# Last partial sum of the first MLP in two passes: the context tokens, then the latents

## The chip, the cores and the metric

The kernel runs on one core of a Trainium2 chip. The core has a matrix engine (TensorE, PE in the rows, with PEld for its weight loads), VectorE (DVE), ScalarE (ACT), GpSimd (POOL) and SyncE (SP), which here issues the loads from memory. The engines work side by side; each takes its own instructions strictly in the order in which they stand in its queue, and they wait for each other through semaphores. The metric is device time in microseconds (us), the median of a few runs.

## The reference, cut to what matters

Two layers over 512 latent tokens and 256 context tokens of width 1024. The first layer's token mixer is a state-space mixer (SSD), the second's a neighbourhood attention in which the latents also read the context.

```python
# layer 0 ends, for the latents x and for the context ctx:
h2 = modulate(rmsnorm(t, g[2]), m[3], m[4])
t  = t + m[5] * rmsnorm(square(relu(h2 @ w1)) @ w2, g[3])       # t is x, or ctx
# layer 1 begins:
h  = modulate(rmsnorm(x,   g[0]), m_lat[0], m_lat[1])
hc = modulate(rmsnorm(ctx, g[0]), m_ctx[0], m_ctx[1])
q, k, v    = h  @ w_qkv                                         # latents
qc, kc, vc = hc @ w_qkv                                         # context: kc and vc are read by the latents
```

## The kernel before

Activations stand with the channels on the partitions: `ya` and `xa` (sub-layer output and residual stream) are 128 x 8 blocks x 768 columns, of which columns 0 to 511 are the latents and 512 to 767 the context (`SEG`, `PARTS`). Every product is made of three matmuls, high part by high part, low by high and high by low (`hh`/`hl`, `ah`/`al` are the two parts of the activations, `wh`/`wl` those of the weights). A weight unit of 128 x 1024 is loaded by SP (`wload`, L112) into one of three buffers and split by ACT (`wh`, L119) and DVE (`wl`, L120) into one of two buffers for each part.

The MLP goes over four quarters `c` of the hidden width: eight hidden blocks (L902), then the second matrix (L954), whose partial sums are added into `ya` by DVE (L960). An accumulator `acc` holds 768 columns, and there are two of them, so the matmuls of one output block can't begin before L960 has emptied the accumulator of the block two before it. In the last quarter each of the eight output blocks also feeds `sums.add`: ACT squares (L299, L306), a scaling by ACT (L389), a product by DVE (L305), and three running sums `syy`, `ssqy`, `sxy` on POOL (L309). After the eighth block `after0` follows:

- `sums.factors` adds over the channels by matmuls with ones (L263), and makes two normalising factors on small row tiles: `R` of the MLP's output, then `r` of the new stream, each by a chain of DVE and ACT instructions (L321, L246 to L250, L334 to L338) that ends in `rows` (L250), a matmul that spreads the row over the partitions (L274) and a copy into `syy` or `sxy` (L275).
- For each of the eight blocks, latents and context: `ya *= R`, `xa += ya` (L351, L352; three of the eight blocks on POOL), then scale and shift into `hh` and `hl`. For the context that is L356 and L358 on DVE and L357 on ACT; for the latents L999 and L1003 on DVE and L1000 and L1002 on ACT (in another column order).

Two chunks of modulation weights (`mod_chunk`, L169, with transposes L186) are worked in meanwhile. The attention then begins with pair `p == 0`: six tiles of values V (four of latents, two of the context; L1174) and the queries Q (L1170) in one loop over the weight halves `q` and blocks `k`, then keys (L1048).

The order within each engine's queue is set when the program is built, by a list scheduler that follows the program's order as priority, with exceptions marked `tc.high_priority()`. On the chip it is fixed.

Two other places already work in passes over columns: the SSD output projection (L144 with L872 in the place of L960), which does the context's 256 columns of all eight blocks, then the latents' 512, with `factors` and the norm of the context (`join`: L351, L352, L377, L378) running during the second pass; and the last MLP, in two halves of 256.

Of the kernel before, what the change touches and what calls it, by code (L numbers as in the profile page):

```python
# [10 lines left out]
ALU = mybir.AluOpType  # L11
AX = mybir.AxisListType

P = 128
D = 1024
KB = D // P
LAT = 512
CTX = 256
T = LAT + CTX
NCH = T // P  # L20
# [31 lines left out]
def trunk(ctx: ExitStack, tc: tile.TileContext, a, out, dbg=None, stop=None):  # L52
# [183 lines left out]
    def scaled(name, l, n, i, plus1):  # L236

        t = const.tile([P, KB, 2], F32, name=name)
        for o in (0, 4):
            scaled_half(t, l, n, i, plus1, o)  # L240
        return t
# [155 lines left out]
    hh, hl = h_tiles()  # L397
# [583 lines left out]
    def between0(c, o, mp):  # L981
        if c == 2 and o == KB - 1:
            G3[0] = scaled("G3", 0, 3, 5, False)

    def after0(i):

        nonlocal hh, hl
        A4 = scaled("A4", 1, 0, 1, True)
        hh, hl = h_tiles()
        sums.factors((0, 1, 2))  # L990
        for k in range(KB):
            for s, sl in enumerate(PARTS):
                sh = mod(1, 0, s)
                add_block(k, ya, xa, sums.R(sl), sl)
                b = ya[:, k, sl]
                if s == 1:
                    modulate(k, b, xa[:, k, sl], sums.r(sl), A4, sh, s, hh[:, k, sl], hl[:, k, sl])
                    continue
                dve.scalar_tensor_tensor(b, xa[:, k, sl], A4[:, k, s:s + 1], sums.r(sl), ALU.mult, ALU.mult)  # L999
                act.activation(b, b, AF.Identity, bias=sh[:, k:k + 1], scale=1.0)  # L1000
                for (bv, _), (_, hv), (_, lv) in zip(slots(b), slots(hh[:, k, sl]), slots(hl[:, k, sl])):
                    act.activation(hv, bv, AF.Copy)  # L1002
                    dve.tensor_tensor(lv, bv, hv.bitcast(F32), ALU.subtract)  # L1003

    segs1 = [(0, LAT, 0), (LAT, T + 2, LAT)]
    mlp(0, SEG, segs1, [segs1[1:], segs1[:1]], [(0, T)], [(0, 10), (0, 11)] + [(1, ch) for ch in (0, 1, 2, 3, 6, 7, 8, 9)], hh, hl, ya, xa, G3,
        between0, after0)
    for ch in (4, 5):
        mod_chunk(1, ch)
# [9 lines left out]
    with tc.tile_pool(name="na", bufs=1) as na:  # L1019
# [138 lines left out]
        for p in range(8):  # L1158
            even = p % 2 == 0
            acc = sps("a")  # L1160
            if p == 0:

                vacc = [sps("a"), sps("a"), sps("sc"), sps("sc"), sps("pt"), sps("yp")]
                ws = wqk.next()
                for q in range(2):
                    w = wv.next()
                    for k2 in range(4):
                        k = q * 4 + k2
                        for j, (ww, xx) in enumerate(((0, hh), (0, hl), (1, hh))):
                            pe.matmul(acc, lhsT=ws[ww][:, k * P:(k + 1) * P], rhs=xx[:, k, :LAT],  # L1170
                                      start=k == 0 and j == 0, stop=k == KB - 1 and j == 2)
                        for i in range(NCH):
                            for n, (xx, ww) in enumerate(((hh, 0), (hh, 1), (hl, 0))):
                                pe.matmul(vacc[i][:, :256], lhsT=xx[:, k, i * P:(i + 1) * P], rhs=w[ww][:, k2 * 256:k2 * 256 + 256],  # L1174
                                          start=k == 0 and n == 0, stop=k == KB - 1 and n == 2)
                for i in range(NCH):
                    v_out(0, vacc[i], i, 1)
            else:
                gemm([acc], SEG[:1], 3 if even else 0, 6 if even else 4)

            Q = [na.tile([P, LAT], F32R, tag=f"q{q}", name=f"q{q}", bufs=2) for q in range(2)]
            Q += qlow[p % 2]
            for o, i, n in ((0, 64, 448), (448, 0, 64)):
                for par in range(2):
                    own = half(par)
                    for to in (own, half(1 - par)):
                        act.activation(Q[par][to, o:o + n], acc[own, i:i + n], AF.Copy, scale=0.125)
                    dve.scalar_tensor_tensor(Q[2 + par][own, o:o + n], acc[own, i:i + n], 0.125, Q[par][own, o:o + n].bitcast(F32),
                                             ALU.mult, ALU.subtract)
            accs = [sps("a"), sps("a")]  # L1190
            gemm(accs, SEG, 0, 11 if even else 5)

            K = [na.tile([P, 896], F32R, tag=f"k{q}", name=f"k{q}", bufs=2) for q in range(2)]
            for acc, k0, n in zip(accs, (0, 640), (512, 256)):
                for par in range(2):
                    own = half(par)
                    act.activation(K[par][own, k0:k0 + n], acc[own, :n], AF.Copy)
                    dve.tensor_tensor(K[par][half(1 - par), k0:k0 + n], acc[own, :n], K[par][own, k0:k0 + n].bitcast(F32), ALU.subtract)
            for k in K:
                pool.tensor_copy(k[:, 512:640], k[:, :128].bitcast(F32))  # L1200
            step(1000)
            pending = attend(p, Q, K)
            if even and p:
                values_of(p)
# [164 lines left out]
```

## Time and profile before

| | |
|---|---|
| median of 3 runs | 2187.4 us (2185.53 to 2195.42) |
| profiled execution | 2191.73 us, its span 2189.9 us |
| busy: PE, PEld | 2073.0 us (95%), 1733.5 us (79%) |
| busy: DVE, ACT, POOL | 1278.6 us (58%), 1008.4 us (46%), 514.3 us (23%) |
| mean granted clock of TensorE | 0.975 |

The span runs from the first to the last instruction; 1.8 us of the profiled execution's time lie outside it. Times in the rows below count from the span's start. Matmuls overlap, so the step from one start to the next says how long one takes, and its own length is longer.

### The profile page before, as it was taken

To read this page: it belongs to the slowest core of one execution; us is meant where nothing else is said; L and a number is where in the kernel's file an instruction comes from. 1 tells how busy PE (TensorE), PEld (TensorE's weight loads), DVE (VectorE), ACT (ScalarE), POOL (GpSimd) and SP (SyncE) were. 2 spreads that over 40 slices of the span, in tenths; PEclk is the share of its full clock that TensorE was granted. 3 is DMA by queue.
4 is the path that set the end of the run, shared out by engine and by line. 5 is a ranking of instruction groups with operands and counts; after the bars stand their busy time and mean duration, and the time that the engine had idled before them with its cause. 6 is when DMAs were issued, how large, how long until landed. Compare 5 with 4: busy or idle time off the path is not lost.

```text
span 2189.9 us, 32496 instructions
## 1 busy us (share of the span) xinstructions
PE 2073.0 (95%) x12848; PEld 1733.5 (79%) x12848; DVE 1278.6 (58%) x2023; ACT 1008.4 (46%) x1751; POOL 514.3 (23%) x486
## 2 busy tenths in 40 slices
PE   6999998999999888999999999889999989999996
PEld 3777876878878766888888888668898768889895
DVE  5657968576683687314334244488777664345356
ACT  4565756567473553213223133356556643323244
POOL 0004435254451462000000001633222260000004
PEclk8999999999999999999999999989999989999998
DMA  6446758357676422333333111321111114222233
GB/s 253 135 152 187 234 158 238 115 173 221 192 200 235 156 74 85 107 114 116 116 116 114 59 59 68 106 78 50 56 54 54 49 50 155 95 97 87 97 107 115
DMA packets 93868, 269.72 MB, mean 123 GB/s; under 512 B 13074, under 2 KB 21652, under 8 KB 93716
## 3 DMA queue, kind: packets, MB, share of 16 engines
q1 hardware_dynamic: 85268, 242.47, 34.0%
q0 software_dynamic: 8448, 25.18, 4.4%
q8 instruction: 101, 1.65, 0.3%
q14 instruction: 51, 0.42, 0.1%
HBM read 244.27 MB, written 23.33 MB: 122 GB/s over the span
## 4 chain that ended last, share of the span: by engine, by line
PE 79%; DVE 9%; ACT 4%; DMA 3%; issue 2%; POOL 2%; SPq 0%; DVEq 0%; ACTq 0%; POOLq 0%
PE acc L902 21%; PE acc L144 21%; PE acc L954 20%; PE a L1048 4%; DMA E<-crow 2%; PE s L169 2%; PE a L1059 2%; PE yp L1134 1%; PE s L629 1%; DVE wl L120 1%; PE s L708 1%; PE pt L1119 1%; PE s L724 1%; PE s L263 1%; ACT wh L119 1%
## 5 line engine op out<-in xcount | busy, mean ns | idle before, releaser
L119 ACT ACTIVATE wh<-raw 128x1024 fp32r<-128x1024 f32 (+1 forms) x241 | 254.2, 1055 | 686.7 <-PE acc L954 309.7
L120 DVE TENSOR_TENSOR wl<-raw,wh 128x1024 fp32r<-128x1024 f32 (+1 forms) x241 | 301.9, 1253 | 255.1 <-ACT wh L119 248.6
L144 PE MATMUL acc<-hh,wh 128*128 128x512 f32 (+1 forms) x976 | 286.2, 370 | 7.8 <-ACT wh L119 3.0
L144 PE MATMUL acc<-hl,wh 128*128 128x512 f32 (+1 forms) x976 | 264.1, 346 | 0.5 <-DVE hl L762 0.5
L144 PE MATMUL acc<-hh,wl 128*128 128x512 f32 (+1 forms) x976 | 262.6, 344 | 2.0 <-DVE wl L120 2.0
L902 PE MATMUL acc<-hh,wh 128*128 128x258 f32 (+2 forms) x1024 | 242.8, 317 | 9.5 <-ACT hh L377 9.5
L954 PE MATMUL acc<-ah,wh 128*128 128x512 f32 (+1 forms) x832 | 247.4, 347 | 4.1 <-DVE ya L960 4.0
L902 PE MATMUL acc<-hl,wh 128*128 128x258 f32 (+2 forms) x1024 | 241.8, 314 | 3.9 <-DVE hl L378 3.8
L954 PE MATMUL acc<-ah,wl 128*128 128x512 f32 (+1 forms) x832 | 244.5, 343 | 0.8 <-DVE wl L120 0.8
L954 PE MATMUL acc<-al,wh 128*128 128x512 f32 (+1 forms) x832 | 244.8, 344 | 0.0
L902 PE MATMUL acc<-hh,wl 128*128 128x258 f32 (+2 forms) x1024 | 240.8, 313 | 0.0
L144 PEld LDWEIGHTS acc<-hh,wh 128*128 128x128 f32 (+1 forms) x976 | 155.2, 190 | 60.9 <-issue 38.3
L902 PEld LDWEIGHTS acc<-hh,wh 128*128 128x128 f32 x1024 | 160.9, 191 | 33.5 <-issue 11.5
L309 POOL TENSOR_TENSOR syy<-syy,last 128x512 f32<-128x512 f32 (+2 forms) x24 | 38.3, 1596 | 585.6 <-ACT last L299 585.5
L144 PEld LDWEIGHTS acc<-hh,wl 128*128 128x128 f32 (+1 forms) x976 | 153.7, 190 | 27.5 <-DVE wl L120 2.5
L902 PEld LDWEIGHTS acc<-hl,wh 128*128 128x128 f32 x1024 | 161.2, 191 | 17.9 <-DVE hl L378 5.9
L144 PEld LDWEIGHTS acc<-hl,wh 128*128 128x128 f32 (+1 forms) x976 | 154.2, 190 | 25.3 <-DVE hl L762 1.1
L902 PEld LDWEIGHTS acc<-hh,wl 128*128 128x128 f32 x1024 | 161.8, 191 | 11.6 <-DVE wl L120 0.4
L954 PEld LDWEIGHTS acc<-ah,wh 128*128 128x128 f32 x832 | 139.4, 189 | 32.7 <-issue 13.1
L954 PEld LDWEIGHTS acc<-ah,wl 128*128 128x128 f32 x832 | 139.6, 189 | 21.9 <-DVE wl L120 1.0
L954 PEld LDWEIGHTS acc<-al,wh 128*128 128x128 f32 x832 | 139.5, 189 | 20.0
L960 DVE TENSOR_TENSOR ya<-ya,acc 128x768 f32<-128x768 f32 (+2 forms) x56 | 40.6, 726 | 196.1 <-PE acc L954 196.1
(320 smaller groups left out, 3813.0 us busy)
## 6 DMA issues: line engine op xcount, KB each, us to landing
raw<-in_w_dram SPq DMA_DIRECT2D x136, 512.0 KB, 3.4
mraw<-in_modw_dram SPq DMA_DIRECT2D x72, 512.0 KB, 3.3
raw<-in_win_dram SPq DMA_DIRECT2D x48, 512.0 KB, 4.0
E<-crow SPq DMA_DIRECT2D x96, 256.0 KB, 5.0
eb<-erow POOLq DMA_DIRECT2D x96, 128.0 KB, 5.5
raw<-in_wout_dram SPq DMA_DIRECT2D x24, 512.0 KB, 3.7
raw<-in_modw_dram SPq DMA_DIRECT2D x8, 1024.0 KB, 17.8
raw<-in_wqk_dram SPq DMA_DIRECT2D x16, 512.0 KB, 3.3
```

Of the source, the lines that this page charges most:

```text
L119: act.activation(wh[:, :n], raw[:, :n], AF.Copy)
L120: dve.tensor_tensor(wl[:, :n], raw[:, :n], wh[:, :n].bitcast(F32), ALU.subtract)
L144: pe.matmul(acc[:m, s0:s1], lhsT=ww[:, i * m:(i + 1) * m], rhs=xx[:, k, s0:s1], start=first and i == 0 and j == 0, stop=last and i == len( ...
L169: mm = pe.matmul(ps[32 * j:32 * j + 32, hf * 256:hf * 256 + 256], lhsT=cact[:, 8 * kg + 2 * j:8 * kg + 2 * j + 32], rhs=raw[:, j * 256:j * ...
L263: pe.matmul(ps[32 * j:32 * j + 32], lhsT=ones[:, :32], rhs=t[i], start=i == 0, stop=i == len(t) - 1)
L309: pool.tensor_tensor(t[:, s0:s1], t[:, s0:s1], d, ALU.add)
L629: pe.matmul(ps, lhsT=btok[:, d, c], rhs=xw.rearrange("p e q -> p (e q)"), start=True, stop=True)
L902: pe.matmul(acc[:, d0:d0 + s1 - s0], lhsT=ww[wi], rhs=xx[:, k, s0:s1], start=k == 0 and j == 0, stop=k == KB - 1 and j == 2)
L954: pe.matmul(acc[:, s0:s1], lhsT=ww[:, k * P:(k + 1) * P], rhs=xx[:, s0:s1], start=k == 0 and j == 0, stop=k == KB - 1 and j == 2)
L960: dve.tensor_tensor(y, y, acc[:, p0:p1], ALU.add)
L1048: pe.matmul(acc[:, :s1 - s0], lhsT=ws[ww][:, k * P:(k + 1) * P], rhs=xx[:, k, s0:s1], start=k == 0 and j == 0, stop=k == KB - 1 and j == 2)
L1059: pe.matmul(acc, lhsT=xx[:, k, i * P:(i + 1) * P], rhs=w[ww][:, sl], start=k == 0 and n == 0, stop=k == KB - 1 and n == 2)
```

## The change

`after0` is called twice in layer 0. The last quarter's second matrix is done first for the 256 context columns of all eight output blocks, then for the 512 latent columns; its eight weight units are loaded and split a second time. After the first pass, the context's factors and norm are issued, after the second the latents'. `factors` is issued with priority. In the attention's first loop, the two context tiles of V are computed first in each half of the weights.

```diff
@@ -982,28 +982,32 @@
         if c == 2 and o == KB - 1:
             G3[0] = scaled("G3", 0, 3, 5, False)
 
+    A4 = [None]
+
     def after0(i):
 
         nonlocal hh, hl
-        A4 = scaled("A4", 1, 0, 1, True)
-        hh, hl = h_tiles()
-        sums.factors((0, 1, 2))
+        if i == 0:
+            A4[0] = scaled("A4", 1, 0, 1, True)
+            hh, hl = h_tiles()
+        with tc.high_priority():
+            sums.factors(((2,), (0, 1))[i])
         for k in range(KB):
-            for s, sl in enumerate(PARTS):
+            for s, sl in ((1 - i, PARTS[1 - i]),):
                 sh = mod(1, 0, s)
                 add_block(k, ya, xa, sums.R(sl), sl)
                 b = ya[:, k, sl]
                 if s == 1:
-                    modulate(k, b, xa[:, k, sl], sums.r(sl), A4, sh, s, hh[:, k, sl], hl[:, k, sl])
+                    modulate(k, b, xa[:, k, sl], sums.r(sl), A4[0], sh, s, hh[:, k, sl], hl[:, k, sl])
                     continue
-                dve.scalar_tensor_tensor(b, xa[:, k, sl], A4[:, k, s:s + 1], sums.r(sl), ALU.mult, ALU.mult)
+                dve.scalar_tensor_tensor(b, xa[:, k, sl], A4[0][:, k, s:s + 1], sums.r(sl), ALU.mult, ALU.mult)
                 act.activation(b, b, AF.Identity, bias=sh[:, k:k + 1], scale=1.0)
                 for (bv, _), (_, hv), (_, lv) in zip(slots(b), slots(hh[:, k, sl]), slots(hl[:, k, sl])):
                     act.activation(hv, bv, AF.Copy)
                     dve.tensor_tensor(lv, bv, hv.bitcast(F32), ALU.subtract)
 
     segs1 = [(0, LAT, 0), (LAT, T + 2, LAT)]
-    mlp(0, SEG, segs1, [segs1[1:], segs1[:1]], [(0, T)], [(0, 10), (0, 11)] + [(1, ch) for ch in (0, 1, 2, 3, 6, 7, 8, 9)], hh, hl, ya, xa, G3,
+    mlp(0, SEG, segs1, [segs1[1:], segs1[:1]], SEG[::-1], [(0, 10), (0, 11)] + [(1, ch) for ch in (0, 1, 2, 3, 6, 7, 8, 9)], hh, hl, ya, xa, G3,
         between0, after0)
     for ch in (4, 5):
         mod_chunk(1, ch)
@@ -1161,15 +1165,21 @@
             if p == 0:
 
                 vacc = [sps("a"), sps("a"), sps("sc"), sps("sc"), sps("pt"), sps("yp")]
-                ws = wqk.next()
                 for q in range(2):
                     w = wv.next()
+                    ws = ws if q else wqk.next()
+                    for i in (4, 5):
+                        for k2 in range(4):
+                            k = q * 4 + k2
+                            for n, (xx, ww) in enumerate(((hh, 0), (hh, 1), (hl, 0))):
+                                pe.matmul(vacc[i][:, :256], lhsT=xx[:, k, i * P:(i + 1) * P], rhs=w[ww][:, k2 * 256:k2 * 256 + 256],
+                                          start=k == 0 and n == 0, stop=k == KB - 1 and n == 2)
                     for k2 in range(4):
                         k = q * 4 + k2
                         for j, (ww, xx) in enumerate(((0, hh), (0, hl), (1, hh))):
                             pe.matmul(acc, lhsT=ws[ww][:, k * P:(k + 1) * P], rhs=xx[:, k, :LAT],
                                       start=k == 0 and j == 0, stop=k == KB - 1 and j == 2)
-                        for i in range(NCH):
+                        for i in range(4):
                             for n, (xx, ww) in enumerate(((hh, 0), (hh, 1), (hl, 0))):
                                 pe.matmul(vacc[i][:, :256], lhsT=xx[:, k, i * P:(i + 1) * P], rhs=w[ww][:, k2 * 256:k2 * 256 + 256],
                                           start=k == 0 and n == 0, stop=k == KB - 1 and n == 2)
```

Two places in the queues. The first is on DVE. Before, in the last quarter of the MLP, the emptying of one accumulator (L960), a weight split (L120) and the product of the sums (L305) follow each other, block after block:

```order
L305 TENSOR_TENSOR sxy_6161<-xa_6158,ya_6159 128x768
L960 TENSOR_TENSOR ya_6159<-ya_6159,acc_11073 128x768
L120 TENSOR_TENSOR wl_11205<-raw_11202,wh_11204 128x1024
L305 TENSOR_TENSOR last1_6162<-xa_6158,ya_6159 128x768
L960 TENSOR_TENSOR ya_6159<-ya_6159,acc_11137 128x768
L120 TENSOR_TENSOR wl_11269<-raw_11266,wh_11268 128x1024
L305 TENSOR_TENSOR last1_6162<-xa_6158,ya_6159 128x768
```

With the change, this stands in the second pass, where the accumulators of latent blocks 1, 2 and 3 are acc_11433, acc_11472 and acc_11511 (that of block 0, acc_11397, is emptied before the context's second factor; acc_11511 takes the buffer of acc_11433):

```order
L351 TENSOR_TENSOR ya_6159<-ya_6159,syy_6160 128x256
L120 TENSOR_TENSOR wl_11554<-raw_11551,wh_11553 128x1024
L358 SCALAR_TENSOR_TENSOR hl_11322<-ya_6159,modc_91,hh_11321 128x256 x2
L352 TENSOR_TENSOR xa_6158<-xa_6158,ya_6159 128x256
L305 TENSOR_TENSOR sxy_6161<-xa_6158,ya_6159 128x512
L356 SCALAR_TENSOR_TENSOR ya_6159<-xa_6158,A4_11318,sxy_6161 128x256
L960 TENSOR_TENSOR ya_6159<-ya_6159,acc_11433 128x512
L358 SCALAR_TENSOR_TENSOR hl_11322<-ya_6159,modc_91,hh_11321 128x256
L960 TENSOR_TENSOR ya_6159<-ya_6159,acc_11472 128x512
L305 TENSOR_TENSOR last1_6162<-xa_6158,ya_6159 128x512 x2
L960 TENSOR_TENSOR ya_6159<-ya_6159,acc_11511 128x512
```

The last context blocks' scale and shift (L356, L358), a weight split and the first latent product now stand in front of the L960 that empties the accumulator of latent block 1. In front of these rows, and behind the `rows` (L250) of the context's second factor, stand one more L120, seven L356 and five L358.

The second place is on PE, at the end of the MLP. Before: the matmuls that spread the second factor (L274, from `rows`), the transposes of the modulation, then the first of V, in which context and latent tiles take turns (pt and yp hold context tiles, sc and a latent ones):

```order
L169 MATMUL acc_11722<-raw_11741,cact_86 32x256 x4
L274 MATMUL s_11572<-rows_6164,sel_81 128x256
L274 MATMUL s_11575<-rows_6164,sel_81 128x256
L274 MATMUL s_11578<-rows_6164,sel_81 128x256
L186 MATMUL acc_11686<-consts_77,row_11711 128x128 x2
L186 MATMUL acc_11686<-consts_77,row_11715 128x128 x2
L186 MATMUL acc_11722<-consts_77,row_11747 128x128 x2
L186 MATMUL acc_11722<-consts_77,row_11751 128x128 x2
L1174 MATMUL pt_11793<-wh_11803,hh_11521 128x256
L1174 MATMUL pt_11793<-wl_11804,hh_11521 128x256
L1174 MATMUL yp_11794<-wh_11803,hh_11521 128x256
```

With the change, with L1175 for the context tiles of V:

```order
L274 MATMUL s_11728<-rows_6164,sel_81 128x256
L169 MATMUL acc_11850<-raw_11857,cact_86 32x256 x4
L169 MATMUL acc_11850<-raw_11863,cact_86 32x256 x4
L169 MATMUL acc_11850<-raw2_11869,cact_86 32x256 x4
L274 MATMUL s_11743<-rows_6164,sel_81 128x256
L274 MATMUL s_11746<-rows_6164,sel_81 128x256
L186 MATMUL acc_11814<-consts_77,row_11839 128x128 x2
L1175 MATMUL pt_11921<-wh_11925,hh_11321 128x256
L1175 MATMUL pt_11921<-wl_11926,hh_11321 128x256
L1175 MATMUL pt_11921<-wh_11925,hl_11322 128x256
L186 MATMUL acc_11814<-consts_77,row_11843 128x128 x2
```

The context tiles come first, and they, too, stand behind the L274 of the latents' second factor; there are two L274 for each factor instead of three.

## Rows read from the trace of the kernel before

**Rows 1.** Stretches: us, busy by engine (instructions), granted clock, DMA share, GB/s.

```profile
1336.65:1404.50 67.85, 67.85 (x387) 58.73 (x389) 27.77 (x26) 28.83 (x38) 35.81 (x18) 1.00 0.17 55
1404.50:1424.90 20.40, 10.16 (x106) 5.23 (x106) 15.38 (x21) 6.35 (x12) 12.61 (x12) 0.71 0.58 206
1424.90:1462.05 37.15, 29.16 (x183) 24.75 (x183) 34.95 (x68) 21.88 (x50) 12.71 (x11) 0.84 0.25 70
730.00:745.00 15.00, 12.23 (x100) 11.43 (x100) 10.92 (x15) 12.63 (x21) 10.86 (x10) 1.00 0.38 128
```

**Rows 2.** Chain that ended last, 1330 to 1500: start, us, what.

```profile
1424.48 0.42 DVE rows L250
...
1433.51 0.79 PE pt L1174 x2
```

**Rows 3.** Context's instructions on DVE, 1424 to 1462: busy us, mean ns.

```profile
L356 DVE SCALAR_TENSOR_TENSOR ya<-xa,A,sxy 128x256 f32<-128x256 f32 x8 | 5.2, 671 | 0.0
...
L358 DVE SCALAR_TENSOR_TENSOR hl<-ya,modc,hh 128x256 fp32r<-128x256 f32 x8 | 4.2, 527 | 0.0
...
L351 DVE TENSOR_TENSOR ya<-ya,syy 128x256 f32<-128x256 f32 x4 | 2.2, 550 | 0.0
...
L352 DVE TENSOR_TENSOR xa<-xa,ya 128x256 f32<-128x256 f32 x4 | 1.7, 417 | 0.0
```

**Rows 4.** PE in time, SSD output projection: start, us, [idle before <- releaser].

```profile
744.15 0.39 PE L144 MATMUL acc<-yh,wl 128*128 128x256 f32 x1 [0.26 <-DVE wl L120]
...
747.40 0.38 PE L144 MATMUL acc<-yh,wl 128*128 128x256 f32 x1 [0.25 <-DVE wl L120]
...
751.93 0.62 PE L263 MATMUL s<-syy,ones 128*32 128x256 f32 x2 [1.75 <-POOL syy L309]
...
753.35 0.50 PE L144 MATMUL acc<-yh,wh 128*128 128x512 f32 x1
...
772.09 0.40 PE L144 MATMUL acc<-yh,wl 128*128 128x512 f32 x1
777.99 1.19 PE L274 MATMUL s<-rows,sel 32*128 32x256 f32 x2 [5.51 <-DVE rows L250]
```

**Rows 5.** POOL's running sums by form, 734 to 753: busy us, mean ns.

```profile
L309 POOL TENSOR_TENSOR sxy<-sxy,last 128x256 f32<-128x256 f32 x6 | 10.3, 1715 | 0.0
L309 POOL TENSOR_TENSOR ssqy<-ssqy,last 128x256 f32<-128x256 f32 x6 | 5.5, 918 | 0.0
L309 POOL TENSOR_TENSOR syy<-syy,last 128x256 f32<-128x256 f32 x6 | 5.1, 857 | 18.7 <-ACT last L299 18.7
```

**Rows 6.** PE in time, the same projection behind the idle time of 5.51 us.

```profile
779.71 0.63 PE L144 MATMUL acc<-yl,wh 128*128 128x512 f32 x1
...
784.83 0.54 PE L144 MATMUL acc<-yl,wh 128*128 128x512 f32 x1
...
785.44 0.39 PE L144 MATMUL acc<-yh,wh 128*128 128x512 f32 x1
...
789.88 0.39 PE L144 MATMUL acc<-yl,wh 128*128 128x512 f32 x1
```

**Rows 7.** One line's instructions, 1424 to 1462: ns min/median/max, first and last start.

```profile
L356 DVE SCALAR_TENSOR_TENSOR ya<-xa,A,sxy x8: 472/480/1555, 1431.4 to 1455.9; 128x256 f32<-128x256 f32 x8
```

**Rows 8.** DVE by form, 1336 to 1404.5: weight splits; busy us, mean ns.

```profile
L120 DVE TENSOR_TENSOR wl<-raw,wh 128x1024 fp32r<-128x1024 f32 x7 | 8.5, 1218 | 0.0
```

**Rows 9.** DVE in time, SSD output projection.

```profile
787.08 0.68 DVE L305 TENSOR_TENSOR last<-xa,ya 128x512 f32<-128x512 f32 x1
...
811.54 0.69 DVE L872 TENSOR_TENSOR ya<-ya,acc 128x512 f32<-128x512 f32 x1 [1.27 <-PE acc L144]
...
828.35 1.49 DVE L250 SCALAR_TENSOR_TENSOR rows<-rt,rows 64x256 f32<-64x256 f32 x1
```

**Rows 10.** PE in time: the keys' first matmul, and the last MLP's second half.

```profile
1462.05 0.50 PE L1048 MATMUL a<-hh,wh 128*128 128x512 f32 x1 [1.53 <-DVE v L1072]
...
2157.66 0.55 PE L954 MATMUL acc<-ah,wh 128*128 128x256 f32 x1 [3.99 <-DVE ya L960]
```

## Prediction

> **What bounds the kernel now.** The page puts PE at 95% of the span, so time comes only out of places where PE waits or runs at its lower clock. I read the busy time by stretch first, and in it the seam between the first MLP and the attention [rows 1]. Three stretches show it. The last quarter's second matrix keeps PE busy for all of 67.85 us at granted clock 1.00: nothing is to be won there, only lost. Then come 20.40 us in which PE works for 10.16, in small matmuls, while the two factors are formed. Then 37.15 us with PE busy for 29.16 and DVE for 34.95: here DVE is the bound. The chain of waits gives the marks: the second factor's row is made at 1424.48 on DVE, the first V matmul starts at 1433.51 [rows 2], and the keys begin at 1462.05 [rows 10]. The instructions by line say how much of DVE's work in the last stretch is the context's: 5.2 + 4.2 + 2.2 + 1.7 = 13.3 us [rows 3].
>
> The change takes those 13.3 us out of the last stretch, and pays by cutting the one stretch without a gap in two. The nearest rows for that are in the same trace: the SSD output projection already does 256 context columns and then 512 latent columns, with the same sums, factors and norm inside.
>
> **The change, part by part.** There are as many matmuls and columns as before. At the upper clock a 512-column matmul steps by 0.2337 us (19 steps from 785.44 to 789.88, [rows 6]); half of that for 256 columns is 0.117. A unit of 24 matmuls takes 2.80 us in the first pass and 5.61 in the second; eight of each are 67.3, against 67.85.
>
> *First pass.* Each block has three sums on POOL, 1.715 + 0.918 + 0.857 = 3.49 us of records that overlap a little [rows 5]. In the projection the pace is 3.25 us a block, from one wait for `wl` to the next [rows 4], above PE's 2.80. The first three blocks run before POOL's queue pushes back, so 3 x 2.80 + 5 x 3.25 = 24.7. The extra eight weight units (loads, L119, L120) lie inside that pace, as there; at the start the third unit's split must wait for a weight buffer that PE now frees every 2.80 us, about one L119, +1.0. In the eighth block PE meets the ones-matmul for `syy`, which waits for POOL; the projection waited 1.75 us and a little more for `ssqy` [rows 4]. I take 2.5, because here it stands in the middle of the block and not behind it. First pass 28.2, against a third of 67.85, 22.6: **+5.6**.
>
> *Second pass.* 8 x 5.61 against 45.2: -0.3. PE breaks off for the context's L263 and L274: in the projection, 66 matmuls lie between 753.35 and 772.32 (the last start plus a step), 18.97 us for 15.42 [rows 4]: **+3.5**. For the second L274 the projection waited 5.51 us [rows 4]. Here the factor has three DVE instructions fewer and no part of `join` ahead of it, so I take **+2.7** (bounds 0 and 5.5).
>
> The largest term is the one that the order shows. Between the L250 of the context's second factor and the L960 that empties latent block 1's accumulator, DVE has two splits (2 x 1.22, [rows 8]), eight L356 at 0.44 (0.48 of record, [rows 7], with a small overlap), seven L358 of the same length, an L351 and L352 of 256 columns (0.76 together), an L305 (0.68, [rows 9]) and some 0.5 of waiting for the spread row (an L274 with its record of 1.19, [rows 4], and a copy behind it, less the first split, which lies in that time): 2.4 + 3.5 + 3.1 + 0.8 + 0.7 + 0.5 = 11.0, and with the L960 itself 0.69 (that of the like L872, [rows 9]) 11.7. PE has in that time the L274, about 0.8, and 18 matmuls of block 2, 4.2. Then block 3 needs that accumulator: **+6.7** of waiting. That such a wait comes about is shown at the last MLP, where PE stood 3.99 us for an L960 held behind L351 and L352 of the first half [rows 10]. Bounds: 0, if DVE gets there in time, and 8.
>
> After its 5.51 us without work PE ran at the lower of its two levels: from 779.71 to 784.83 twelve steps of 0.427 us, and at the upper one behind [rows 6]: 13 x (0.427 - 0.2337) = 2.5. I count it once, behind the wait for L960: **+2.5** (bounds 0 and 5, if the wait for L274 brings it too). In the last block the ones-matmuls for the latents again wait for POOL, and break in twice: **+2.0**, from the 1.75 above.
>
> The Trainium skill, TensorE: Matmul & The Clock Gate, section "A second HAM failure mode: psum-queue depth-cycling", says that a PE which idles briefly between groups of matmuls while it cycles through accumulators can swing between its two clocks again and again. The trace does not agree here: from 730 to 745, with such waits in each block, the granted clock was 1.00 [rows 1]. By the rule the first pass would run at the lower level (third rival); by the row it costs nothing, and the sum goes by the row.
>
> Together the second pass ends 5.6 - 0.3 + 3.5 + 2.7 + 6.7 + 2.5 + 2.0 = **22.7 us later** than now.
>
> *The chain of the factors.* From the last matmul to the second `rows` it is 20.4 us now (1404.50 to 1424.90, [rows 1]); in the projection, with the latents alone, it took from 811.54 to 829.84, 18.3 [rows 9]. The modulation's matmuls stay, so I take the middle, **-1.0**. The context tiles of V don't fill this hole: in PE's queue they stand behind the second L274.
>
> *The last stretch.* It now takes 1462.05 - 1424.48 = 37.6 us [rows 2, 10]. Without the context, DVE's 34.95 become 21.7, and PE becomes the bound: 24 Q matmuls of 0.2337 and 144 V matmuls of 0.117 are 22.5. The first V matmul now comes 9.0 us behind the row (1433.51); with the context gone, the latents' first block should come some 1.5 earlier, at 7.5, by one L356 as slow as the first (1.555, [rows 7]). The 24 context matmuls that are ready by then (2.8) lie in that wait, the rest takes 19.7, and the keys wait 1.53 for the V tiles to be emptied as now [rows 10]. 28.7: gain 8.9. Those first matmuls run at the lower clock, as now, and the L186 are mixed in, so I keep **-8.5** (bounds -6 and -13.3, all of DVE's part).
>
> Sum: 22.7 - 1.0 - 8.5 = +13.2 us on the profiled execution's 2191.7, 2204.9. The median of the runs is 4.3 lower: 2187.4 + 13.2 = **2200.6 us**, 0.6% slower.
>
> **The rivals.** *DVE gets to the L960 in time* (not slower by over 0.5%). The place is the same accumulator; if the context's L356 and L358 run where DVE is idle, PE loses neither the 6.7 nor the 2.5, and the time is 2187.4 + 4.0 = 2191.4. It decides when DVE needs less than PE's 5 us between L250 and that L960. For it: in the projection, with the like join, no such wait stands in the trace. Against it: there DVE empties block 1 before the second factor, here after the scale of all eight context blocks.
>
> *The last stretch gives back all 13.3.* DVE is busy for 34.95 of 37.15 us there [rows 1]; if what leaves it comes off whole, the sum is +8.4, 2195.8: no change that can be told. Against it: PE needs its 22 us behind the first `hh`.
>
> *The first pass at the lower clock.* 192 matmuls of 256 columns at half of 0.427, 41.0 us in place of 28.2: another +12.8, 2213.4. Against it the clock of 1.00 [rows 1].
>
> The change does what it says, by the order, except that the context tiles of V come first without coming earlier.
>
> **How the numbers follow.** The forecast gets 0.55, with a range of its own from 2194 to 2208 (the wait for L960 from 2 to 8, the last stretch from -6 to -12); the first rival 0.22, the second 0.15, the third 0.08. A measurement of this kernel can tell about 0.5%, 11 us. Slower than 2198.3 come out four fifths of the forecast's share, 0.44, the third rival's 0.08 and a little of the second, 0.03: 0.55. Faster by 11 us would need both of the first rivals at their lower ends and cheaper passes: 0.06. Same 0.39. For 8 times in 10 the range runs from 2187, where the first rival has a cheap second factor too, to 2211.
>
> **What would show it.** Right, if in the new profile PE waits for an L960 (DVE `ya`) at the fourth block of the second pass for 4 us or more, if the second pass ends 18 to 26 us later than 1404.5, if the first pass takes 26 to 30, and if from the second `rows` to the keys it is 27 to 31 us. Wrong, if no such wait is there, if the first pass stays at 23, or if the last stretch falls under 25.

## Result and the profile after

The changed kernel takes **2209.05 us**, median of 5 runs (2206.19 to 2212.89), against 2187.4 (5 runs, 2185.38 to 2195.42): ratio **1.0087**, 95% interval 1.007 to 1.0103. It is slower, by 0.87%. (The ratio is formed from the runs of both kernels; the two medians alone would give 1.0099.) The forecast was 2200.6, so 8.5 us of the loss were not in the sum.

Stretches of the profiled execution after (2212.89 us, span 2211.0): first pass, second pass, from its last L960 to the second factor's `rows`, from there to the keys. They answer to [rows 1].

```profile
1338.14:1367.80 29.66, 25.46 (x199) 23.53 (x198) 21.93 (x28) 18.71 (x33) 18.96 (x18) 1.00 0.43 142
1367.80:1431.88 64.08, 55.28 (x216) 39.88 (x218) 40.56 (x61) 27.76 (x45) 31.92 (x25) 0.92 0.20 64
1431.88:1446.57 14.69, 7.65 (x84) 2.71 (x83) 10.80 (x20) 4.82 (x10) 9.19 (x8) 0.85 0.79 276
1446.57:1482.13 35.56, 29.06 (x180) 25.89 (x181) 26.36 (x49) 20.36 (x48) 13.04 (x8) 0.87 0.27 74
```

Before, PE was busy for all of the last sum. Now it is idle for 4.2 us of the first pass and 8.8 of the second, and the second runs at a mean granted clock of 0.92. What PE waited for in the two passes, by the list of waits (us in total, times, longest):

```profile
PE acc L954 <- DVE ya L960: 5.1, 1, 5.1
PE s L263 <- POOL syy L309: 3.6, 2, 2.9
PE s L274 <- DVE rows L250: 2.9, 1, 2.9
PE acc L954 <- ACT wh L119: 1.2, 2, 0.8
```

PE in time: the three large waits, a matmul behind the longest, and the keys.

```profile
1365.04 0.62 PE L263 MATMUL s<-syy,ones 128*32 128x256 f32 x2 [2.85 <-POOL syy L309]
...
1386.78 0.69 PE L274 MATMUL s<-rows,sel 32*128 32x256 f32 x2 [2.92 <-DVE rows L250]
...
1398.51 0.77 PE L954 MATMUL acc<-ah,wh 128*128 128x512 f32 x1 [5.11 <-DVE ya L960]
...
1399.50 0.63 PE L954 MATMUL acc<-ah,wl 128*128 128x512 f32 x1
...
1404.19 0.58 PE L954 MATMUL acc<-al,wh 128*128 128x512 f32 x1
...
1482.13 0.47 PE L1052 MATMUL a<-hh,wh 128*128 128x512 f32 x1 [2.83 <-DVE v L1076]
```

From 1399.50 to 1404.19 there are 11 steps of 0.426 us: the lower level, as in [rows 6]. DVE, in the time in which PE stood for L960, was at work on the context:

```profile
1386.31 0.42 DVE L250 SCALAR_TENSOR_TENSOR rows<-rt,rows 32x256 f32<-32x256 f32 x1
1386.75 1.23 DVE L120 TENSOR_TENSOR wl<-raw,wh 128x1024 fp32r<-128x1024 f32 x1
1387.98 1.28 DVE L356 SCALAR_TENSOR_TENSOR ya<-xa,A,sxy 128x256 f32<-128x256 f32 x3
...
1394.29 1.23 DVE L120 TENSOR_TENSOR wl<-raw,wh 128x1024 fp32r<-128x1024 f32 x1 [1.13 <-ACT wh L119]
...
1397.67 0.69 DVE L960 TENSOR_TENSOR ya<-ya,acc 128x512 f32<-128x512 f32 x1
```

The queue is the one that the order showed, 11.4 us from L250 to L960. The chip did what was read from the order; that this was the cost of the change is another matter.

### The profile page after: what moved, and what is told of

It reads as the page before. It is cut to its first block, busy times and chain, and to the rows that moved or that the text cites. A ratio compares the mean times of both kernels' runs of the same rounds, so it can differ in the third digit from the quotient of the medians.

```text
span 2211.0 us, 32632 instructions
## 1 busy us (share of the span) xinstructions
PE 2081.3 (94%) x12848; PEld 1735.4 (78%) x12848; DVE 1300.4 (59%) x2059; ACT 1020.6 (46%) x1779; POOL 525.5 (24%) x504
## 4 chain that ended last, share of the span: by engine, by line
PE 61%; DVE 6%; POOL 3%; ACT 3%; issue 2%; DMA 1%; SPq 0%; DVEq 0%; ACTq 0%; POOLq 0%
PE acc L902 20%; PE acc L954 19%; PE acc L144 8%; PE a L1052 4%; PE a L1063 2%; PE yp L1138 1%; PE s L169 1%; POOL sxy L309 1%; PE pt L1123 1%; DVE wl L120 1%; POOL syy L309 1%; DVE ya L351 1%; POOL ssqy L309 1%; ACT wh L119 1%; DVE xa L352 1%
## 5 line engine op out<-in xcount | busy, mean ns | idle before, releaser
L119 ACT ACTIVATE wh<-raw 128x1024 fp32r<-128x1024 f32 (+1 forms) x249 | 262.6, 1055 | 684.4 <-PE acc L954 301.1
L120 DVE TENSOR_TENSOR wl<-raw,wh 128x1024 fp32r<-128x1024 f32 (+1 forms) x249 | 312.7, 1256 | 263.9 <-ACT wh L119 257.4
L954 PE MATMUL acc<-ah,wh 128*128 128x512 f32 (+1 forms) x832 | 260.3, 350 | 10.4 <-DVE ya L960 9.1
L954 PE MATMUL acc<-al,wh 128*128 128x512 f32 (+1 forms) x832 | 257.4, 346 | 0.0
L954 PE MATMUL acc<-ah,wl 128*128 128x512 f32 (+1 forms) x832 | 256.6, 346 | 0.9 <-DVE wl L120 0.8
L902 PEld LDWEIGHTS acc<-hh,wh 128*128 128x128 f32 x1024 | 161.4, 192 | 33.6 <-issue 11.9
L954 PEld LDWEIGHTS acc<-ah,wh 128*128 128x128 f32 x832 | 145.0, 190 | 42.0 <-issue 15.0
L309 POOL TENSOR_TENSOR syy<-syy,last 128x512 f32<-128x512 f32 (+1 forms) x30 | 40.1, 1336 | 577.5 <-ACT last L299 577.4
L954 PEld LDWEIGHTS acc<-ah,wl 128*128 128x128 f32 x832 | 145.1, 190 | 22.8 <-DVE wl L120 1.3
L954 PEld LDWEIGHTS acc<-al,wh 128*128 128x128 f32 x832 | 145.2, 190 | 21.0 <-issue 1.2
L960 DVE TENSOR_TENSOR ya<-ya,acc 128x256 f32<-128x256 f32 (+2 forms) x64 | 41.7, 653 | 180.5 <-PE acc L954 180.4
## 6 DMA issues: line engine op xcount, KB each, us to landing
raw<-in_modw_dram SPq DMA_DIRECT2D x8, 1024.0 KB, 17.7
```

The lines of the kernel that those rows point to most:

```text
L119: act.activation(wh[:, :n], raw[:, :n], AF.Copy)
L120: dve.tensor_tensor(wl[:, :n], raw[:, :n], wh[:, :n].bitcast(F32), ALU.subtract)
L309: pool.tensor_tensor(t[:, s0:s1], t[:, s0:s1], d, ALU.add)
L902: pe.matmul(acc[:, d0:d0 + s1 - s0], lhsT=ww[wi], rhs=xx[:, k, s0:s1], start=k == 0 and j == 0, stop=k == KB - 1 and j == 2)
L954: pe.matmul(acc[:, s0:s1], lhsT=ww[:, k * P:(k + 1) * P], rhs=xx[:, s0:s1], start=k == 0 and j == 0, stop=k == KB - 1 and j == 2)
L960: dve.tensor_tensor(y, y, acc[:, p0:p1], ALU.add)
```

## Experiments

Each run is compared with the kernel before, on the same chip; the median of the kernel before was between 2187.4 and 2192.5 us on these, so that ratios can be compared down the table, and medians only within some us. As each program shifts against the others by some us ahead of the seam, I read the seam by itself, from the first matmul of the last quarter's second matrix: the passes (to the last L960), the chain (to the second factor's L250), the last stretch (to the keys). Each seam is read from one execution. Kernels with the same code in the passes agree there within 0.1 us (before, e2 and f3; the changed kernel, e3 and e8); the chain of before and that of e2, the same code too, differ by 0.6.

| run | passes | chain | last | sum | ratio, 95% interval |
|---|---|---|---|---|---|
| before | 68.0 | 20.0 | 37.6 | 125.6 | |
| f3, before, latents off POOL | 68.0 | 17.3 | 38.6 | 123.9 | 1.0000, 0.9987 to 1.0013 |
| e2, order of V alone | 68.0 | 19.4 | 39.1 | 126.5 | 1.0015, 1.0001 to 1.003 |
| f2, cut alone | 70.3 | 19.1 | 41.0 | 130.4 | 1.0012, 0.9996 to 1.0029 |
| f4, factors behind block 0, norm held | 83.5 | 17.7 | 42.0 | 143.1 | 1.0081, 1.0064 to 1.0098 |
| e7, factors at once, norm held | 82.9 | 18.8 | 41.0 | 142.6 | 1.0080, 1.0057 to 1.0102 |
| changed kernel | 93.7 | 14.7 | 35.6 | 144.0 | 1.0087, 1.007 to 1.0103 |
| e1, L960 first | 93.8 | 14.7 | 34.3 | 142.8 | 1.0091, 1.007 to 1.0113 |
| e3, old order of V | 93.8 | 14.7 | 35.0 | 143.5 | 1.0076, 1.0054 to 1.0097 |
| e5, norm issued later | 94.5 | 14.8 | 34.3 | 143.5 | 1.0091, 1.0069 to 1.0114 |
| e6, sxy on DVE | 93.7 | 15.1 | 34.3 | 143.1 | 1.0088, 1.0069 to 1.0108 |
| e8, latents off POOL | 93.8 | 13.6 | 33.2 | 140.6 | 1.0085, 1.0064 to 1.0106 |
| f1, norm behind block 2 | 95.1 | 15.2 | 35.6 | 145.8 | 1.0088, 1.0065 to 1.0110 |
| e9, chunks in the MLP | 94.2 | 16.0 | 37.1 | 147.3 | 1.0124, 1.01 to 1.0148 |

**e1, the wait for L960 removed.** In the last quarter:

```
-                            dve.tensor_tensor(y, y, acc[:, p0:p1], ALU.add)
+                            with tc.high_priority() if c == 3 and l == 0 else nullcontext():
+                                dve.tensor_tensor(y, y, acc[:, p0:p1], ALU.add)
```

> The changed kernel, but in the last quarter DVE's L960, which empties an accumulator, is issued at high priority, so that it stands ahead of the context's L356 and L358 in DVE's queue. Theory: the wait of 5.11 us for L960 in the second pass goes, and with it part of the lower clock behind it; 5 to 8 us off the median of 2209.1, so 2201 to 2204. The context's norm ends later, but still in the second pass. Rival: DVE's work is only moved, the context's norm ends late and the stretch behind the second factor grows by what is saved; 2207 to 2210.

2209.37 us: nothing was won. The wait for L960 (L961 in this kernel) is down from 5.1 to 1.1, but the passes take 93.8 us as before. PE's waits in them:

```profile
PE s L263 <- POOL syy L309: 4.3, 2, 2.8
PE s L274 <- DVE rows L250: 3.8, 1, 3.8
PE acc L954 <- ACT wh L119: 1.2, 2, 0.8
PE acc L954 <- DVE ya L961: 1.1, 1, 1.1
PE acc L954 <- DVE wl L120: 1.0, 1, 1.0
```

The sum is 11.4 us against 12.8, and the lower clock came three times in place of twice (behind L263, L274 and the two last waits). The first pass is 1.5 us longer by it and the second 1.4 us shorter, 62.66; but in e3 and e8, which have the passes of the changed kernel, the first pass fell to the lower clock as well, and the second takes 62.60 and 62.69. Compared with these, e1 wins nothing in either pass. My rival said that DVE's work is moved and paid for in the last stretch; it was moved, but was paid for in the same pass.

**e2 and e3, the order of the V tiles.** e2 puts the V loop of the change into the kernel before; e3 takes it out of the changed kernel (this diff; e2's is its reverse):

```
+                ws = wqk.next()
...
-                    for i in (4, 5):
-                        for k2 in range(4):
...
-                        for i in range(4):
+                        for i in range(NCH):
```

> The kernel before with one part of the change alone: the context tiles of V first in the attention's first loop; the last sum in one pass as before. Theory: DVE makes context and latent blocks in turn, and is the bound of that stretch, so the order of PE's V tiles matters little: 0 to 3 us longer, 2187 to 2191. Rival: in the new order PE stands behind the fourth context block while latent blocks are ready; 5 us longer or more, 2193 and up.

> The changed kernel with the old order of the V tiles: two passes and the context normed meanwhile, but all six tiles of a block together. Theory: the context tiles no longer fill the time until the first latent block (PE had 12 to 24 of their matmuls there), so 2 to 5 us longer than the changed kernel: 2211 to 2214. Rival: PE waits for DVE in that stretch anyway, and the order is worth nothing: 2208 to 2210.

e2: 2193.92 against 2190.75, 3.2 us longer, at the edge of the theory's 0 to 3. e3: 2205.69, under both expectations: the theory fell, as the run is not longer than the changed kernel. So that part is worth nothing on top of the passes, and at most 0.3% the wrong way alone.

**e5 and e7, the norm without its early place.** e5 only moves the context's norm behind the second pass in the program's text (its one line is the first diff); e7 holds it there on DVE, ACT and POOL, behind the last instruction of the latents' sums on each:

```
-            for s, sl in ((1 - i, PARTS[1 - i]),):
+            for s, sl in enumerate(PARTS) if i else ():
```

```
+        if not i:
+            return
+        with tc.issue_after(sums.ld), tc.issue_after(sums.la), tc.issue_after(sums.lp):
+            for k in range(KB):
+                for s, sl in enumerate(PARTS):
...
```

> The changed kernel, but only the context's factors are formed between the passes; its residual and norm are issued behind the second pass, with the latents'. Theory: this shows what the cut in two alone costs: first pass +6.9, break-ins and the wait for the second L274 +6, no wait for L960, factors -3 to -5, last stretch as before the change (37.6, DVE the bound): +7 to +11 on 2187.4, so 2194 to 2199, less than the changed kernel, because the norm's early place costs as much as it gives back. Rival: the early norm pays for itself in the last stretch, and without it the time is above that of the changed kernel, 2212 or more.

> The two passes and the context's factors as in the change, but its residual and norm are held, on each engine, behind the last sums of the latents. Theory: the early norm is worth little, because the first latent block of hh and not DVE's total sets the last stretch; the second pass gains 2 to 4 us without the norm inside, the last stretch loses as much: 2206 to 2211. Rival: the early norm is worth the 8.5 us that I put down for it; 2213 to 2217.

e5 (2209.02) did not do what I meant: the scheduler put the norm back into the second pass, in its trace L356 runs on DVE from 1390.57 on. It is one more place for the norm, with the same price, and decides neither expectation. e7 (2209.09) is the run that speaks. Its stretches, cut as those above:

```profile
1334.15:1365.34 31.19, 26.97 (x199) 24.35 (x198) 21.94 (x28) 18.70 (x33) 18.97 (x18) 0.95 0.39 135
1365.34:1417.04 51.70, 50.67 (x216) 36.84 (x218) 28.19 (x35) 24.24 (x37) 29.70 (x22) 1.00 0.21 72
1417.04:1435.79 18.75, 8.27 (x84) 2.74 (x83) 17.17 (x32) 8.10 (x15) 15.63 (x12) 0.74 0.69 245
1435.79:1476.76 40.97, 30.89 (x181) 27.34 (x181) 31.32 (x62) 20.55 (x50) 12.52 (x8) 0.78 0.21 63
```

Without the norm inside, PE works through the second pass almost without a gap, at clock 1.00. The early norm costs 93.7 - 82.9 = 10.8 us there and gives back 59.7 - 50.3 = 9.4 in the chain and the last stretch. Of the 10.8, 7.8 are idle time of PE (13.0 us in the changed kernel's two passes, 5.2 here), the rest are slower steps at the lower clock. My theory holds in the median; in its mechanism it was too low on both sides.

**f2, the cut alone.** The kernel before with the two passes, but both factors formed together behind them (POOL also takes the last context block's sums, so that its rows stay until then); no early norm, old V loop.

```
+        if i == 0:
+            return
...
-    mlp(0, SEG, segs1, [segs1[1:], segs1[:1]], [(0, T)],
+    mlp(0, SEG, segs1, [segs1[1:], segs1[:1]], SEG[::-1],
```

> The kernel before with the cut in two passes alone: both factors are formed together behind the second pass, the norm and the order of the V tiles are those of before. Theory: the first pass keeps the pace of its sums (3.25 us a block) but loses the break-ins of L263 and the lower clock: 27 to 28.5 us; the second pass has nothing in it, 45 to 47; the rest as before, 57.5: 5 to 8 us more than before, 2194 to 2198. The other 7 to 10 us of the cut (82.9 against 68 with the factors in it, 14.9) are the factors' ones-matmuls, spreads and their waits. Rival: the two passes cost their 14.9 us without any factor in them; 2202 or more.

2195.06 us against 2188.93; the ratio is 1.0012 (0.9996 to 1.0029), so that the difference can't be told from none:

```profile
1340.21:1367.30 27.09, 25.72 (x202) 24.30 (x201) 21.88 (x27) 19.59 (x33) 17.65 (x17) 1.00 0.45 139
1367.30:1410.49 43.19, 43.19 (x188) 34.34 (x190) 23.83 (x24) 21.35 (x30) 32.04 (x23) 1.00 0.29 96
```

The median is as expected. The two passes together take 70.3 us, less than the 72 to 75.5 expected and 2.2 more than the one before; what follows them takes 60.1 in place of 57.5, so that the whole seam is 4.8 us longer than before. The pace of POOL's sums is felt in the first pass, but with no L263 in the way PE goes on into the second (its first matmul of 512 columns starts at 1365.22, ahead of the last emptied accumulator of the context), where POOL catches up.

**f4, the context's factors behind the first latent block**, where POOL is long done; else e7:

```
+            if done[0] == KB + 1:
+                with tc.issue_after(sums.mm), tc.high_priority():
+                    sums.factors((2,))
...
```

> The run with the norm held to the end, but with the context's factors formed behind the first block of the latents' pass, where POOL has long finished its sums, and not inside the last context block. The two passes took 70.3 us with the cut alone and 82.9 with the factors at once. Theory: most of these 12.6 us is the waiting of PE for POOL's last sums (2.86), the lower clock behind it and the break-ins in a half-done block; placed behind a block, they cost 4 to 7 us, the passes take 74 to 78, and the median falls from 2209 to 2201 to 2205. Rival: the ones-matmuls and spreads cost that much wherever they stand; the passes stay at 81 us or more and the median at 2207 to 2211.

2210.7 us; the rival holds. The first pass is down to 27.09 as in f2, but the second takes 56.37. PE in time: the first and last ones-matmuls and the next matmul, then the second L274 and what follows.

```profile
1373.27 0.62 PE L263 MATMUL s<-syy,ones 128*32 128x256 f32 x2
...
1375.98 0.50 PE L954 MATMUL acc<-ah,wh 128*128 128x512 f32 x1
...
1389.96 1.17 PE L274 MATMUL s<-rows,sel 32*128 32x256 f32 x2 [2.87 <-DVE rows L250]
...
1392.08 0.63 PE L954 MATMUL acc<-ah,wh 128*128 128x512 f32 x1
```

2.7 us go for the ones-matmuls, and the second L274 waits 2.87 us for a factor that is late on DVE although no norm is there, and brings the lower clock. Moving the factors moves the wait, from POOL's sums to DVE's row.

**f1, the norm behind the third latent block.** The changed kernel with e1's priority; the norm is issued from the loop over blocks, held behind the sums of block 2.

```
+            if done[0] == KB + 3:
+                with tc.issue_after(sums.ld), tc.issue_after(sums.la), tc.issue_after(sums.lp):
+                    norm0(0)
...
```

> The changed kernel, with the context's residual and norm held on each engine behind the sums of the third latent block (its factors still right behind the first pass), and L960 of the last quarter at high priority. Theory: what the second pass loses to the early norm, 12.4 us against the run with the norm held to the end (64.1 and 51.7), comes from the norm standing between the context's two factors and in front of L960; placed behind, the pass takes 52 to 56 us, while the factors' chain (14.7) and the stretch behind it (35) keep their gain: 8 to 11 us off the changed kernel, 2198 to 2202. Rival: the norm's DVE and POOL work holds up the sums wherever it stands in the pass, which stays at 60 us or more; 2206 to 2210.

2210.86 us; the rival. The second L274 no longer waits, but in the two passes PE stands 4.5 us for L960 (L961 in this kernel) in three places, 2.0 for L120 and 5.2 for POOL's sums.

**e6, sxy on DVE in the context pass.**

```
-                    pool.tensor_tensor(t[:, s0:s1], t[:, s0:s1], d, ALU.add)
+                    eng = dve if n == 1 and self.part and s0 == LAT else pool
+                    eng.tensor_tensor(t[:, s0:s1], t[:, s0:s1], d, ALU.add)
...
```

> The changed kernel, with one of the three running sums of the context pass (sxy, 1.68 us of POOL's 3.3 a block) moved to DVE, which has some 20 us of 29.5 busy there. Theory: POOL sets the pace of the first pass and the wait of 2.85 us at its end; both go, the pass falls from 29.5 to 24 or 25 us and the median from 2209 to 2203 to 2205. Rival: DVE and POOL hold each other up when both read SBUF (an L305 of 512 columns takes 0.69 us alone and 1.25 to 1.78 beside a sum on POOL), DVE now sets the pace, and the pass stays at 28 or more; 2207 to 2210.

2209.4 us, the first pass 31.0, the wait at its end 2.12: the rival. DVE's queue now sets the pace, from one accumulator emptied to the next 3.23 us.

**e8 and f3, the latents' residual on DVE in place of POOL**, in the changed kernel and in the one before (the line of e8; in f3 it ends in `ON_POOL if s else ()`):

```
-                add_block(k, ya, xa, sums.R(sl), sl)
+                add_block(k, ya, xa, sums.R(sl), sl, () if i else ON_POOL)
...
```

> The changed kernel, with the residual (L351, L352) of the latents' blocks 2, 4 and 6 on DVE in place of POOL. Theory: behind the second factor DVE is held up by POOL (L1003 takes 1.86 and 1.65 us beside it and 0.74 alone, L191 1.23 for 8 columns), so the first latent block comes 2 us earlier and the stretch from the second rows to the keys falls from 35.6 to 32 to 34: 2205 to 2207. Rival: DVE has 4 us more to do ahead of that block and nothing is won; 2209 to 2213.

> The kernel before, with the residual of the latents' blocks 2, 4 and 6 on DVE in place of POOL; the context's stay on POOL. In the changed kernel the like took 3.5 us off behind the last sum (chain 14.7 to 13.6, last stretch 35.6 to 33.2). Theory: DVE is the bound of that stretch here (34.95 of 37.15 us), so 4.1 us more work for it eats what fewer hold-ups by POOL give: 2188 to 2193, no change that can be told. Rival: the hold-ups weigh more, 3 to 5 us less than before, 2184 to 2187.

e8's chain and last stretch are 46.8 us against 50.3, the last being 33.2: as expected there; its median, 2209.17, lies in the rival's range, and 3 us can't be told in it. f3: 2189.4 against 2188.93, no change. Nothing tried beats the kernel before.

**e9, chunks 4 and 5 among the MLP's pieces.** They join the list of chunks there, and behind the MLP goes:

```
-    for ch in (4, 5):
-        mod_chunk(1, ch)
```

> The changed kernel, with modulation chunks 4 and 5 computed among the MLP's pieces like the other ten, not behind it. Theory: their L186, L184, L190 and L191 stand ahead of the first latent block of the norm (L191 1.2 us twice); without them the last stretch is 2 to 3 us shorter, and the MLP pays 4 to 6 us for 32 more small matmuls in PE's full stretch: 2209 to 2213. Rival: the first latent block gets 4 us earlier and the matmuls are hidden; 2203 to 2207.

2218.64 us, worse than both expected. Without the modulation's matmuls PE has 4.27 us of work in the 16.03 of the chain, its clock there is 0.59, and in the last stretch 0.81 against 0.87. That makes 3.3 us of the seam; the profiled execution is the fastest of the four (2212.91), and what the others lose beyond it stays open.

## Why the prediction came out right in sign and short in size

**What the loss is made of.** Each step from one run to the next adds one part: the cut alone +2.2 (f2), the factors formed behind each pass +12.6 (e7), the norm at once +10.8: together +25.7 us for the passes. The 12.6 hold, beside the context's factors in the middle, the latents' ones-matmuls, which in e7 break into the last block and in f2 stand behind it. Behind them, e7 is 2.2 longer than before, and the early norm gives back 9.4. Net 18.4; with 1.7 ahead of the seam and 1.0 behind the keys this is the 21.1 us between the two profiles' spans.

**The passes**, +22.7 forecast, +25.7 measured. First pass 26 to 30: 29.66. The wait for L960 over 4 us at the fourth block: 5.11, for 6.7; the lower clock came already behind L274, and the 18 matmuls ahead of that wait took 5.8 us in place of 4.2. The second L274: 2.92, for 2.7. The second pass ends 27.4 us later than 1404.5, outside the 18 to 26 of my sign; counted from the start of the seam it is 25.7. The terms of the cut and of the factors, 5.6 - 0.3 + 3.5 + 2.0 = 10.8, stand against 14.9 in e7: short by 4, of which 1.5 is the lower clock that the wait for L263 brings in e7. The waits for the second L274 (none is left in e7) and for L960 with the clock behind it, 2.7 + 6.7 + 2.5 = 11.9, stand against the 10.8 of the early norm. The sizes are near, but what I took from the largest, that the loss hangs on it, was wrong. I put it down to one instruction in one place of DVE's queue. e1 took that away, f1 and e5 moved the norm, and the passes stayed at 93.8 to 95.1. So the early norm's price belongs to its work on DVE and POOL during the passes, whichever wait shows it. It isn't that DVE is full: it is busy for 40.6 of the 64.1 us. What PE waits for stands behind other work in a queue that is taken in order, or behind POOL's sums. This is argued from the waits of e1 and f1; no run moved DVE's or POOL's share of the context's residual by itself, so how the price divides between the two stays open.

**The first rival** fell with that: in e1 DVE did come to L960 nearly in time, and the 9.2 us did not come back. **The third** (the first pass at the lower clock) has the nearest figure, 2213.4, but not its mechanism: the granted clock of the first pass is 1.00.

**The chain and the last stretch** are where the step failed. Forecast: -1.0 and -8.5; measured -5.3 and -2.0. For the chain I took the middle between now and the projection; e7 shows that it is the context's work in DVE's queue between the two factors that made it long (18.8 with it, 14.7 without). For the last stretch I let the first latent block come 7.5 us behind the second `rows` and made PE the bound from there. In the changed kernel the latents' scale is L1003 and their high and low parts are L1006 and L1007. PE's first matmul with a latent block, and its wait for the low part:

```profile
1455.75 0.39 PE L1184 MATMUL sc<-wh,hh 128*128 128x256 f32 x1 [1.39 <-ACT hh L1006]
...
1458.57 0.39 PE L1184 MATMUL a<-wh,hl 128*128 128x256 f32 x1 [1.58 <-DVE hl L1007]
```

DVE in time, the row and the way to the first `hl`:

```profile
1446.57 0.41 DVE L250 SCALAR_TENSOR_TENSOR rows<-rt,rows 64x256 f32<-64x256 f32 x1
...
1451.45 1.23 DVE L191 TENSOR_TENSOR modc<-modt,cols 128x8 f32<-128x8 f32 x1
1452.61 1.86 DVE L1003 SCALAR_TENSOR_TENSOR ya<-xa,A,sxy 128x512 f32<-128x512 f32 x1
1454.40 0.18 DVE L190 TENSOR_REDUCE modt<-acc 128x8 f32<-128x32 f32 x1
1454.50 1.65 DVE L1003 SCALAR_TENSOR_TENSOR ya<-xa,A,sxy 128x512 f32<-128x512 f32 x1
1456.07 1.24 DVE L191 TENSOR_TENSOR modc<-modt,cols 128x8 f32<-128x8 f32 x1
1457.24 0.74 DVE L1003 SCALAR_TENSOR_TENSOR ya<-xa,A,sxy 128x512 f32<-128x512 f32 x1
1457.90 1.42 DVE L1007 TENSOR_TENSOR hl<-ya,hh 128x448 fp32r<-128x448 f32 x4
```

The first latent matmul comes 9.2 us behind the row, not 7.5: 1.7 more. PE then stands 1.58 us for the first `hl`, 11.3 behind the row, and does the next 14 matmuls at the lower clock, in 3.7 us for 2.1: 1.6 more. At the far end the keys wait 2.83 us for DVE to empty the V accumulators, where I had kept 1.53: 1.3 more. That explains 6.2 of the 6.9 us between the 28.7 of my terms and 35.6; the rest I have not pinned down. The context had left DVE, but POOL's part of the residual had not, and beside it L1003 and L191 are slow; with the latents off POOL (e8) the same `hl` stands at 9.0 and the stretch at 33.2. Taking the modulation away in its place (e9) leaves DVE waiting 2.43 us for POOL's L352, the `hl` at 9.9 and the stretch at 37.1. The sign I gave for this step, 27 to 31 us, was missed at 35.6.

The median lies 8.5 us above the forecast, 1 us above the forecast's own range (2194 to 2208) and inside the one for 8 times in 10 (2187 to 2211). Of this the profile gives 5.2 to the seam (18.4 for 13.2) and 2.7 to the shifts around it, which no step of mine had.

## What to carry to other kernels

Cutting a stretch in which the matrix engine never waits can be cheap by itself (here 2.2 us in the passes, and a time that can't be told from the one before); what is put into the cut was dear here, because a reduction with a long chain on another engine breaks it twice, once for its sums and once for its result. Before moving work under such a stretch, look at what will stand, in each queue, in front of the instructions that the matrix engine waits for, and not at how busy those engines are in the mean: removing the wait that showed brought up others here (e1, f1, f4, e6). Time a held version, with the early result but without its use, against the change: it splits price and return, which the change alone shows only as their difference.

## What the runs showed of the hardware

**The same wait may or may not bring the lower clock.** Behind a wait of PE for the same L263, the changed kernel stayed at the upper level and e1 fell, with steps of 0.12 and 0.21 us for 256 columns. First a matmul behind the wait of 2.85 us in the changed kernel:

```profile
1366.05 0.28 PE L954 MATMUL acc<-ah,wl 128*128 128x256 f32 x1
1366.16 0.28 PE L954 MATMUL acc<-ah,wh 128*128 128x256 f32 x1
```

then the wait and two matmuls behind it in e1:

```profile
1362.42 0.62 PE L263 MATMUL s<-syy,ones 128*32 128x256 f32 x2 [2.82 <-POOL syy L309]
...
1363.77 0.41 PE L954 MATMUL acc<-ah,wl 128*128 128x256 f32 x1
1363.98 0.41 PE L954 MATMUL acc<-ah,wh 128*128 128x256 f32 x1
```

The pass is 1.5 us longer by it (31.14 against 29.66). By the mean granted clock of the first pass, e9 stayed up as well (1.00, behind a wait of 2.82 us), and e3, e5, e7, e8 and f1 fell (0.95, behind 2.82 to 2.86 us): the length of the wait does not tell them apart. Nor does it tell how long the lower level lasts: behind the same wait of 5.1 us for L960, the changed kernel and e9, which had stayed up in the first pass, did 13 matmuls at the lower level, and e3 and e8, which had fallen, 5 and 6. The two passes of e8:

```profile
1337.40:1368.54 31.14, 26.94 (x199) 24.47 (x198) 21.94 (x28) 18.71 (x33) 18.95 (x18) 0.95 0.40 135
1368.54:1431.23 62.69, 53.89 (x216) 38.93 (x218) 42.56 (x61) 27.70 (x45) 33.37 (x25) 0.95 0.18 66
```

Together they take 93.8 us, as in the changed kernel (29.66 and 64.08): what the first pass lost, the second did not lose again. A sum can hold the price of one such wait only as a chance.

**DVE and POOL hold each other up.** An L305 of 512 columns took 0.69 us where POOL was idle, and 1.52 in the median beside POOL's sums. The L191 took 1.24 us for 8 columns in the changed kernel and 0.16 in e8, where POOL does not work on the latents' residual (minimum, median, maximum in ns; the changed kernel, then e8):

```profile
L191 DVE TENSOR_TENSOR modc<-modt,cols x2: 1234/1239/1244, 1451.5 to 1456.1; 128x8 f32<-128x8 f32 x2
```

```profile
L191 DVE TENSOR_TENSOR modc<-modt,cols x2: 159/160/160, 1450.6 to 1453.1; 128x8 f32<-128x8 f32 x2
```

L960, which reads one of its inputs from PSUM, took at most 0.69 in all eight blocks of the second pass, four of them beside POOL's sums. The Trainium skill, SBUF — State Buffer, section "Who interferes with whom", says that a DVE instruction with two inputs in SBUF contends with a GpSimd instruction that reads SBUF, and that one with at most one SBUF input, outside the modes that use both ports, does not. The traces agree in all three cases. In my sum DVE's records were taken from the trace of before as if they were prices of the instruction alone.
